# A decoder layer on one NeuronCore: the memory's row factors and mLSTM's gates laid out by DMAs of GpSimd's queue

## The chip, the cores and the metric

The kernel runs on one NeuronCore of a Trainium2 chip, in float32. The metric is the device time of one execution in microseconds (us); a run's time is compared as the median of several.

## What is computed

One decoder layer over 256 tokens of 2048 channels, and a memory of 256 tokens:

```python
h = rms_norm(x, mix_norm_g)
p = h @ w_in                                   # 2048 x 6408, split into ten parts
y_lru = rg_lru_branch(lru_x, lru_z, ...)       # 512 channels
y_ml = mlstm_branch(ml_u, ml_o, ml_z, ml_i, ml_f, ...)  # 4 heads of 192
y_mo = moba_branch(mo_q, mo_k, mo_v, mo_z)     # 6 heads of 128
x = x + concatenate([y_lru, y_ml, y_mo]) @ w_out
x = x + memory_cross_attention(rms_norm(x, xa_norm_g), rms_norm(mem, mem_norm_g), wq, wkv, wo)
return rms_norm(x, final_norm_g)
```

Two pieces matter here. The memory's norm is a factor for each memory token, `rsqrt(mean(mem^2) + eps)`. And mLSTM has an input gate `ig` and a forget gate `lf = log_sigmoid(f)` for each token and head: with `b = cumsum(lf)` and the running maximum of `ig - b`, each score is multiplied by `exp(ig - b - maximum)` of its key and query, and the output is divided by at least `exp(-m)`, where `m` is `b` plus that maximum.

## The kernel before, in words

**The matrix products.** All weights are read once, in 172 chunks, in the order of the table `GROUPS`: lx, u0, u4, lz0, o0, o1, lz2, q0 to q4, k0 to k4, z0, v0, v1, z1, z2, out0 to out3, ck0, ck2, cq0, cq2, cv, wo0 to wo3. A group of 512 or 384 columns has eight chunks of two 128-row tiles, one of 256 columns four chunks of four. `load(i)` fetches chunk i on SyncE's queue (line 172). `split(i)` makes two parts of it: `wh` by ScalarE (line 197) and the remainder `wl` by VectorE (line 198, by the helper of line 148). `mm(i)` multiplies on TensorE: for groups of kind C by pairs of lines 260 (wh) and 261 (wl), for kind X by lines 282 to 284, of which 283 reads wl.

**The order.** The loop of lines 1100 to 1124 writes every engine's order. For chunk i it calls `split(i + 4)`, the next `load`, `mm(i)`, then `done(group)` behind a group's last chunk, then `step()`. `done` puts generators into `queue`, and `step` takes one piece of the generator in front; `urgent` puts one in front, `bg` at the end. `yield HARD` ends a step without anything else. So all work beside the products stands on each engine's queue in the place of the chunk in whose step it was written, and each engine goes through its queue in order.

**The memory's factor.** `mem_stats` (1025) loads `memT`, channels on partitions, in eight pieces. `square` (393) squares each on ScalarE (401), and GpSimd adds the squares up (402, 404). `stats("m")` (417) sums over the partitions by two matmuls with ones (426), takes the power on GpSimd (359), and brings the factors into a row that all partitions have: a diagonal `yt` by VectorE (430), a matmul with ones (433), a copy `rrow` by ScalarE (436). `ck_evac` multiplies by it through `fold` (444): ScalarE copies half of the accumulators to `ev`, VectorE adds the other half, and GpSimd multiplies by `rrow` (451). For x's factor, `xrow_load` and `xrow_square` take row sums from `x` itself. The tile `yt` is used by `x1_evac` too: ScalarE's squares of the output tiles go there (852).

**The gates.** `o_evac` writes the eight gate columns to `if`, tokens on partitions (549). `ml_gates` (555) stands at the end of the queue when o0 is done, and takes its turn in q2. VectorE computes the logarithms in a chain of small instructions on 128 x 8 (561 to 564). Four transposes on TensorE (586, 587) give rows of 4 partitions, one a head, by 256 tokens; VectorE scans them (589, 591); four more transposes (600, 601) bring them back to columns `acol` and `enb`. The negated running maximum goes as two parts to `nrow`, and each head's `scores` (651) broadcasts it to all partitions by two matmuls with `sel` (654), the rows of which choose the head.

**Around the gates.** `ml_conv` (531) has one step a channel tile with three VectorE instructions (537), on `w`; `lru_z` (501) folds the LRU's gate, and ScalarE's Silu (507) reads what GpSimd's fold wrote.

Of the kernel before, what the change touches and what calls it, by code (L numbers as in the profile page):

```python
# [105 lines left out]
def kernel(ctx: ExitStack, tc: tile.TileContext, xT, memT, x, mem, ws, vec_d, lw_d, fg_d, out):  # L106
# [283 lines left out]
    rrow = {}  # L390
    sq = {}

    def square(which, j):

        t = staged[which, j]
        if j == 0:
            sq[which] = small("mask", 512)
            S.activation(sq[which], t.rearrange("p a b -> p (a b)"), AF.Square)
        else:
            q = small("yt", 512)  # L400
            S.activation(q, t.rearrange("p a b -> p (a b)"), AF.Square)  # L401
            G.tensor_tensor(sq[which], sq[which], q, OP.add)  # L402
        if j == 7:
            G.tensor_tensor(sq[which][:, :256], sq[which][:, :256], sq[which][:, 256:], OP.add)

    ssqx = small("ssqx", 2, 2)
    xrow = {}

    def xrow_load(i):
        xrow[i] = big(i + 1, 1024)  # L410
        t, c = i // 2, i % 2 * 1024
        nc.sync.dma_start(xrow[i], x[t * 128:t * 128 + 128, c:c + 1024])

    def xrow_square(i):
        S.activation(xrow[i], xrow[i], AF.Square, accum_out=ssqx[:, i // 2, i % 2:i % 2 + 1])

    def stats(which):
        r = small(f"rstd_{which}", 2)
        rstd[which] = r
        if which == "x":  # L420
            V.reduce_sum(r, ssqx, axis=AX.X)
            rstd_of(r, r, D, RMS_EPS)
        else:
            p = ps()
            for t in range(2):
                P.matmul(p[:, t:t + 1], sq[which][:, t * 128:t * 128 + 128], ones[:, 0:1], start=True, stop=True)
            rstd_of(r, p[:, 0:2], D, RMS_EPS)
        d = small("yt", 512)[:, :256].rearrange("p (a b) -> p a b", a=2)
        for t in range(2):
            V.tensor_scalar(d[:, t, :], ident, r[:, t:t + 1], None, op0=OP.mult)  # L430
        yield
# [122 lines left out]

    def ml_gates():
        iff = M["if"]
        lf, e = small("lf", 8), small("lf_e", 8)
        f = iff[:, :, 4:8]
        e3 = e.rearrange("p (a b) -> p a b", a=2)
        lf3 = lf.rearrange("p (a b) -> p a b", a=2)  # L560
        stt(e3, f, -1.0, f, OP.mult, OP.max)
        S.activation(e, e, AF.Exp, scale=-1.0)
        log1p(lf, e, "lf")
        stt(lf3, f, 0.0, lf3, OP.min, OP.subtract)
        cmask = small("mask", 512)[:, :384]
# [5 lines left out]
        w = big(6, 4, 256)[:4]  # L571
        sel = selp.tile([128, 4, 128], F32R, name="sel")
        ones_r = ones[:, :128]
        M["sel"] = sel
        for h in range(4):
            G.affine_select(sel[:, h, :], ones_r, pattern=[[0, 128]], compare_op=OP.is_equal, fill=0.0,
                            base=-h, channel_multiplier=1)
        nrow = [selp.tile([128, 256], F32R, name=f"nrow{i}") for i in range(2)]
        for r in nrow:
            G.memset(r.bitcast(F32), 0.0)  # L580
        M["nrow"] = nrow
        yield HARD
        yield HARD
        p = ps()
        for t in range(2):
            P.transpose(p[:4, t * 128:t * 128 + 128], lf3[:, t, :], ident)
            P.transpose(p[:4, 256 + t * 128:256 + t * 128 + 128], iff[:, t, 0:4], ident)
        cb, av, cm, ncm = (w[:, i, :] for i in range(4))
        V.tensor_tensor_scan(cb, ones[:4, :], p[:4, 0:256], 0.0, op0=OP.mult, op1=OP.add)
        tt(av, p[:4, 256:512], cb, OP.subtract)  # L590
        V.tensor_tensor_scan(cm, ones[:4, :], av, 0.0, op0=OP.mult, op1=OP.max)
        V.tensor_scalar(ncm, cm, -1.0, None, op0=OP.mult)
        tt(cb, ncm, cb, OP.subtract)
        nh, nl = (r[:4, :] for r in M["nrow"])
        V.tensor_copy(nh, ncm)
        tt(nl, ncm, nh.bitcast(F32), OP.subtract)
        yield HARD
        p = ps()
        for t in range(2):
            P.transpose(p[:, t * 8:t * 8 + 4], av[:, t * 128:t * 128 + 128], ident[:4, :4])  # L600
            P.transpose(p[:, t * 8 + 4:t * 8 + 8], cb[:, t * 128:t * 128 + 128], ident[:4, :4])
        p3 = p[:, :16].rearrange("p (a b) -> p a b", a=2)
        acol, enb = small("acol", 2, 4), small("enb", 2, 4)
        V.tensor_copy(acol, p3[:, :, 0:4])
        S.activation(enb, p3[:, :, 4:8], AF.Exp)
        M["acol"], M["enb"] = acol, enb
        yield HARD

# [35 lines left out]
    def ml_heads():  # L644
# [6 lines left out]
        def scores(h):  # L651
            pn = ps()
            for i in range(2):
                P.matmul(pn[:, :256], M["sel"][:, h, :], M["nrow"][i], start=i == 0, stop=i == 1)
            e = small(f"mo_l{h % 3}", 384)
            E[h] = e
            stt(e[:, :256], pn[:, :256], acol[:, 0, h:h + 1], cmask[:, :256], OP.add, OP.add)
            stt(e[:, 256:], pn[:, 128:256], acol[:, 1, h:h + 1], cmask[:, 256:], OP.add, OP.add)
# [366 lines left out]
    def mem_stats():  # L1025
        for j in range(10):
            if j < 8:
                stage_load("m", memT, j)
            if j >= 2:
                square("m", j - 2)  # L1030
# [9 lines left out]
    def done(name, a):  # L1040
# [59 lines left out]
    for i in range(NS):  # L1100
# [94 lines left out]
```

## Time and profile before

| | |
|---|---|
| median of 3 runs | 522.26 us (521.66 to 522.65) |
| profiled execution | 521.88 us, span 520.2 us |
| TensorE busy (matmuls) | 507.9 us, 98% |
| VectorE, ScalarE, GpSimd busy | 338.0, 292.8, 54.8 us |
| TensorE's granted clock | full in all but the last of 40 slices |
| moved by DMAs | 98.74 MB, 190 GB/s in the mean |

In the profile's rows PE is TensorE's matmuls, PEld its weight loads, DVE is VectorE, ACT ScalarE, POOL GpSimd, SP SyncE, and a q behind a name is that engine's queue of DMA issues. A group of rows below is from the timeline: the start in us from the span's start, the time taken in us, the engine, the line of the kernel, the instruction with what it writes and reads, and how often; in brackets how long the engine stood idle before it and who ended that. TensorE's matmuls overlap, so what one costs is read from the start of the next, not from its own length.

### The profile page before, as it was taken

Reading aid. Unit: us, or ns where it says so; the run is one execution under the profiler, and the core shown is the slowest. Engines: PE = TensorE matmul, PEld = TensorE weight load, DVE = VectorE, ACT = ScalarE, POOL = GpSimd, SP = SyncE. Lnnn points to the kernel's source line nnn. Section 1 sums busy time; section 2 is a strip of 40 time slices with the busy share of each in tenths; the row PEclk is TensorE's granted clock in tenths of the full one; section 3 lists DMA queues with packets and bytes.
Section 4 is the critical chain, followed back from the end, with each engine's and each line's share of the span. In section 5 each row is a group of like instructions: output and inputs, shape, how many; then the busy total and the mean of one; then the engine's idle time right before and its main releaser. Section 6 shows DMA issues by size and latency. Waiting matters only on the chain.

```text
span 520.2 us, 7578 instructions
## 1 busy us (share of the span) xinstructions
PE 507.9 (98%) x2814; PEld 448.8 (86%) x2814; DVE 338.0 (65%) x531; ACT 292.8 (56%) x476; POOL 54.8 (11%) x70
## 2 busy tenths in 40 slices
PE   8999999999999999999999999999999999999993
PEld 6999889998988888889988888888888888888883
DVE  5958848895397656548645466654658749637574
ACT  5775477678544333353545755543649467546353
POOL 2800001000132100002000000000132003000000
PEclk9999999999999999999999999999999999999998
DMA  8995635467446544435843465478575527734704
GB/s 274 360 412 180 187 120 167 139 221 230 160 160 178 186 161 163 151 92 183 271 155 121 137 209 179 164 272 325 188 264 174 194 66 259 237 128 129 234 3 161
DMA packets 31077, 98.74 MB, mean 190 GB/s; under 512 B 3520, under 2 KB 3904, under 8 KB 31040
## 3 DMA queue, kind: packets, MB, share of 16 engines
q1 hardware_dynamic: 30896, 98.25, 56.9%
q8 instruction: 22, 0.36, 0.3%
q14 instruction: 15, 0.12, 0.1%
q10 hardware_dynamic: 144, 0.01, 0.0%
HBM read 96.15 MB, written 2.10 MB: 189 GB/s over the span
## 4 chain that ended last, share of the span: by engine, by line
PE 85%; issue 6%; POOL 3%; DVE 3%; DMA 1%; ACT 1%; SPq 1%; POOLq 0%; ACTq 0%; DVEq 0%
PE acc_out L284 5%; PE acc_out L282 5%; PE acc_out L283 5%; PE acc_q L260 4%; PE acc_k L260 4%; PE acc_z L284 4%; PE acc_z L282 4%; PE acc_z L283 4%; PE acc_cq L260 3%; PE acc_lz L260 3%; PE acc_q L261 2%; PE acc_k L261 2%; PE acc_o L283 2%; PE acc_o L282 2%; PE acc_o L284 2%
## 5 line engine op out<-in xcount | busy, mean ns | idle before, releaser
L148 DVE TENSOR_TENSOR wl<-raw,wh 128x1024 fp32r<-128x1024 f32 (+3 forms) x166 | 199.6, 1212 | 111.7 <-ACT wh L197 109.3
L197 ACT ACTIVATE wh<-raw 128x1024 fp32r<-128x1024 f32 (+2 forms) x162 | 161.8, 1013 | 44.5 <-DMA raw<-ws 14.8
L282 PE MATMUL acc_out<-wh,a_y 128*128 128x512 f32 x128 | 50.8, 397 | 0.0
L284 PE MATMUL acc_out<-wh,a_y 128*128 128x512 f32 x128 | 49.9, 390 | 0.0
L283 PE MATMUL acc_out<-wl,a_y 128*128 128x512 f32 x128 | 49.8, 389 | 0.0
L282 PE MATMUL acc_z<-wh,a_x 128*128 128x512 f32 x96 | 39.6, 412 | 0.0
L284 PE MATMUL acc_z<-wh,a_x 128*128 128x512 f32 x96 | 37.6, 391 | 0.0
L283 PE MATMUL acc_z<-wl,a_x 128*128 128x512 f32 x96 | 37.5, 390 | 0.0
L260 PE MATMUL acc_k<-a_x,wh 128*128 128x512 f32 x96 | 34.4, 401 | 0.0
L260 PE MATMUL acc_q<-a_x,wh 128*128 128x512 f32 x96 | 34.1, 398 | 0.0
L451 POOL TENSOR_TENSOR w<-ev,rrow 128x512 f32<-128x512 f32 x11 | 17.5, 1589 | 153.6 <-DVE ev L148 153.6
L284 PEld LDWEIGHTS acc_out<-wh,a_y 128*128 128x128 f32 x128 | 24.0, 188 | 5.2
L283 PEld LDWEIGHTS acc_out<-wl,a_y 128*128 128x128 f32 x128 | 24.1, 188 | 4.7
L282 PEld LDWEIGHTS acc_out<-wh,a_y 128*128 128x128 f32 x128 | 24.1, 188 | 4.6
L261 PE MATMUL acc_k<-a_x,wl 128*128 128x256 f32 x96 | 26.9, 280 | 0.0
L261 PE MATMUL acc_q<-a_x,wl 128*128 128x256 f32 x96 | 26.8, 280 | 0.0
L402 POOL TENSOR_TENSOR mask<-mask,yt 128x512 f32<-128x512 f32 x7 | 10.3, 1473 | 147.1 <-ACT yt L401 147.1
L260 PE MATMUL acc_lz<-a_x,wh 128*128 128x512 f32 x64 | 23.3, 406 | 0.0
L260 PE MATMUL acc_ck<-a_m,wh 128*128 128x512 f32 x64 | 23.1, 403 | 0.0
L260 PE MATMUL acc_cq<-a_h,wh 128*128 128x512 f32 x64 | 22.7, 399 | 0.0
L283 PE MATMUL acc_o<-wl,a_x 128*128 128x392 f32 (+1 forms) x64 | 21.6, 338 | 0.0
L282 PE MATMUL acc_o<-wh,a_x 128*128 128x392 f32 (+1 forms) x64 | 21.6, 337 | 0.0
(302 smaller groups left out, 1187.4 us busy)
## 6 DMA issues: line engine op xcount, KB each, us to landing
raw<-ws SPq DMA_DIRECT2D x138, 512.0 KB, 4.1
raw<-ws SPq DMA_DIRECT2D x24, 384.0 KB, 3.1
w<-x SPq DMA_DIRECT2D x8, 512.0 KB, 6.5
raw<-ws SPq DMA_DIRECT2D x8, 392.0 KB, 3.1
w<-memT SPq DMA_DIRECT2D x8, 256.0 KB, 6.1
out<-xg SPq DMA_DIRECT2D x8, 256.0 KB, 3.0
w<-xT SPq DMA_DIRECT2D x7, 256.0 KB, 6.7
raw<-ws SPq DMA_DIRECT2D x4, 256.0 KB, 5.0
```

The source lines that it names most:

```text
L148: V.tensor_tensor(out, a, b, op)
L197: S.activation(h[:, :kc * n], r[:, :kc * n], AF.Copy)
L260: P.matmul(a[m], h[:, sl], both, start=first, stop=False, skip_group_check=True)
L261: P.matmul(a[m][:, :256], l[:, sl], xh, start=False, stop=last, skip_group_check=True)
L282: P.matmul(o, xh[:, sl], mh, start=first, stop=False)
L283: P.matmul(o, xh[:, sl], ml, start=False, stop=False)
L284: P.matmul(o, xl[:, sl], mh, start=False, stop=last)
L402: G.tensor_tensor(sq[which], sq[which], q, OP.add)
L451: G.tensor_tensor(dst, e, rb(which), OP.mult)
```

## The change

Three things change.

- The memory's row sums are taken as x's were: four loads of `mem` by rows, 512 KB each, into the tiles w1 and w2, squared by ScalarE with its accumulator (`row_load`, `row_square`). `memT` is still loaded for the products.
- The memory's factors go to DRAM and back: GpSimd's queue writes 256 numbers to `d_m`, three steps later it reads them as a row for all partitions into `rrow`. The diagonal and the matmul are left to x alone.
- `ml_gates` no longer waits in `queue`: it is in `side`, and `step` takes one piece of it in every step. Its two changes of layout go through DRAM on GpSimd's queue: the gates to `d_if` and back as four transfers of four heads by 128 single numbers; the scan's results in four such transfers to `d_gates` and back as `acol`. The maximum goes to `d_nrow` and comes back in `nrow` for all 128 partitions and four heads, 512 KB, so `scores` has no matmul for it. `sel` and the two-part `nrow` go.

```diff
@@ the memory's statistics
-    def square(which, j):
...
-            S.activation(q, t.rearrange("p a b -> p (a b)"), AF.Square)
-            G.tensor_tensor(sq[which], sq[which], q, OP.add)
...
+    MROW = (1, 2, 1, 2)
+
+    def row_load(which, src, i, tag):
+        rows[which, i] = big(tag, 1024)
         t, c = i // 2, i % 2 * 1024
+        nc.sync.dma_start(rows[which, i], src[t * 128:t * 128 + 128, c:c + 1024])
+
+    def row_square(which, i):
+        t = rows[which, i]
+        S.activation(t, t, AF.Square, accum_out=ssq[which][:, i // 2, i % 2:i % 2 + 1])
...
+        V.reduce_sum(r, ssq[which], axis=AX.X)
+        rstd_of(r, r, D, RMS_EPS)
+        rr = small("rrow", 256)
+        if which == "m":
+            yield
+            d = drp.tile([2, 128], F32, name="d_m")
+            with nc.allow_non_contiguous_dma(reason="two numbers a token"):
+                G.dma_start(d.rearrange("t p -> p t"), r)
+            yield from idle(3)
+            G.dma_start(rr, d.rearrange("t p -> (t p)")[None, :].to_broadcast([128, 256]))
         else:
-            p = ps()
-            for t in range(2):
-                P.matmul(p[:, t:t + 1], sq[which][:, t * 128:t * 128 + 128], ones[:, 0:1], start=True, stop=True)
...
@@ the gates, behind the logarithms and the mask
+        V.tensor_copy(f, lf3)
+        yield
+
+        d = drp.tile([256, 8], F32, name="d_if")
+        G.dma_start(d.rearrange("(t p) c -> p t c", t=2), iff)
+        yield from idle(3)
+        w = big(6, 5, 256)[:4]
+        w, o = w[:, :2, :], w[:, 2:, :]
+        with nc.allow_non_contiguous_dma(reason="one number each"):
+            for a in range(2):
+                for n in (slice(0, 128), slice(128, 256)):
+                    G.dma_start(w[:, a, n], d[n, 4 * a:4 * a + 4].rearrange("n h -> h n"))
+        yield from idle(4)
...
+        V.tensor_tensor_scan(cb, ones[:4, :], w[:, 1, :], 0.0, op0=OP.mult, op1=OP.add)
...
+        d, dn = drp.tile([256, 8], F32, name="d_gates"), drp.tile([4, 256], F32, name="d_nrow")
+        with nc.allow_non_contiguous_dma(reason="one number each"):
+            for a in range(2):
+                for n in (slice(0, 128), slice(128, 256)):
+                    G.dma_start(d[n, 4 * a:4 * a + 4].rearrange("n h -> h n"), o[:, a, n])
+        G.dma_start(dn, o[:, 2, :])
+        yield from idle(4)
+        ac, nrow = small("acol", 2, 8), selp.tile([128, 4, 256], F32, name="nrow")
+        G.dma_start(ac, d.rearrange("(t p) c -> p t c", t=2))
+        G.dma_start(nrow, dn[None, :, :].to_broadcast([128, 4, 256]))
+        yield from idle(4)
+        enb = small("enb", 2, 4)
+        S.activation(enb, ac[:, :, 4:8], AF.Exp)
...
@@ scores, step, mem_stats, done
-            pn = ps()
-            for i in range(2):
-                P.matmul(pn[:, :256], M["sel"][:, h, :], M["nrow"][i], start=i == 0, stop=i == 1)
+            pn = M["nrow"][:, h, :]
...
+        for g in list(side):
+            if next(g, True):
+                side.remove(g)
...
+        for j in range(8):
+            if j < 4:
+                row_load("m", mem, j, MROW[j])
+            stage_load("m", memT, j)
+            if 2 <= j < 6:
+                row_square("m", j - 2)
+            yield
...
-            bg(ml_gates())
+            side.append(ml_gates())
```

The scratch for DMAs that the program makes itself (`dynamic_dma_scratch_size`) goes from 2048 to 4096 as well.

**VectorE's order in o1.** The rows are from `if`, the gate columns, on; `w` is the convolution's tile, `lf` and its companions the logarithms. Before:

```order
L151 SCALAR_TENSOR_TENSOR if<-acc_o_1018,rstd_x,vec 128x8
L151 SCALAR_TENSOR_TENSOR if<-acc_o_1019,rstd_x,vec 128x8
L148 TENSOR_TENSOR wl_1180<-raw_1095,wh_1179 128x768
L151 SCALAR_TENSOR_TENSOR w_1150<-w_779,vec,w_1150 128x256 x3
L148 TENSOR_TENSOR wl_1204<-raw_1114,wh_1203 128x768
L151 SCALAR_TENSOR_TENSOR w_1150<-w_779,vec,w_1150 128x256 x3
L148 TENSOR_TENSOR wl_1226<-raw_1136,wh_1225 128x768
L151 SCALAR_TENSOR_TENSOR w_1150<-w_779,vec,w_1150 128x256 x3
```

Now, from the same wl on (lines are those of the changed kernel):

```order
L150 TENSOR_TENSOR wl_1183<-raw_1098,wh_1182 128x768
L153 SCALAR_TENSOR_TENSOR lf_e<-if 128x8
L367 TENSOR_SCALAR lf_q<-lf_e 128x8
L368 RECIPROCAL lf_q<-lf_q 128x8
L150 TENSOR_TENSOR lf_s<-lf_e,lf_q 128x8
L150 TENSOR_TENSOR lf_s_1208<-lf_s 128x8
L371 TENSOR_SCALAR lf_q<-lf_s_1208 128x8
L153 SCALAR_TENSOR_TENSOR lf_q<-lf_q,lf_s_1208 128x8 x6
L153 SCALAR_TENSOR_TENSOR lf_q<-lf_q,lf_s 128x8
L375 TENSOR_SCALAR lf<-lf_q 128x8
L153 SCALAR_TENSOR_TENSOR lf<-if,lf 128x8
L566 COPY if<-lf 128x2x4
```

The logarithms, before written in q2, and a copy of them into `if` stand between the wl of o1's fifth chunk and the convolution's next step; behind the copy the order goes on as before.

**GpSimd's order from lz0 to k0.** `w` with `ev` and `rrow` is a fold; `mask`, `sel` and the first `nrow` are the gates' constants. Before:

```order
L451 TENSOR_TENSOR w_1005<-ev,rrow 128x512
L616 MEMSET qh 64x256 x4
L451 TENSOR_TENSOR w_1005<-ev,rrow 128x512
L451 TENSOR_TENSOR w_1582<-ev,rrow 128x512
L567 MEMSET mask 128x384
L569 AFFINE_SELECT mask<-mask 128x256
L569 AFFINE_SELECT mask<-mask 128x128
L576 AFFINE_SELECT sel<-ones 128x128 x4
L580 MEMSET nrow_1648 128x256
L580 MEMSET nrow_1649 128x256
L451 TENSOR_TENSOR w_1582<-ev,rrow 128x512 x2
```

Now (`w_1322` is the gates' tile of four partitions):

```order
L562 MEMSET mask 128x384
L564 AFFINE_SELECT mask<-mask 128x256
L564 AFFINE_SELECT mask<-mask 128x128
L570 DMA d_if<-if 128x2x8
L577 DMA w_1322<-d_if 4x128x1 x4
L609 MEMSET qh 64x256 x4
L590 DMA d_gates<-w_1322 4x128x1 x4
L591 DMA d_nrow<-w_1322 4x256
L445 TENSOR_TENSOR w_1008<-ev,rrow 128x512
L594 DMA acol<-d_gates 128x2x8
L595 DMA nrow<-d_nrow 128x1024
L445 TENSOR_TENSOR w_1638<-ev,rrow 128x512 x3
```

The gates' DMAs stand in front of the memsets of `qh` (half-filled queries that ScalarE completes) and around lz2's fold (`w_1008` behind `d_nrow`); before, that fold had only `qh` in front of it.

**VectorE's order in out3, the memory's factor.** Before:

```order
L148 TENSOR_TENSOR wl_3922<-raw_3826,wh_3921 128x1024
L151 SCALAR_TENSOR_TENSOR a_m_3939<-w_3707,vec,a_m_3939 128x256 x2
L357 TENSOR_SCALAR rstd_m<-ps_3945 128x2
L430 TENSOR_SCALAR yt<-ident,rstd_m 128x128 x2
L148 TENSOR_TENSOR wl_3954<-raw_3852,wh_3953 128x1024
L151 SCALAR_TENSOR_TENSOR a_m_3971<-w_3707,vec,a_m_3971 128x256 x2
L148 TENSOR_TENSOR w_3482<-acc_out_3764,w_3482 128x512
```

Now:

```order
L150 TENSOR_TENSOR wl_3804<-raw_3700,wh_3803 128x1024
L153 SCALAR_TENSOR_TENSOR a_m_3821<-w_3490,vec,a_m_3821 128x256 x2
L412 TENSOR_REDUCE rstd_m<-ssq_m 128x2
L359 TENSOR_SCALAR rstd_m<-rstd_m 128x2
L150 TENSOR_TENSOR wl_3832<-raw_3719,wh_3831 128x1024
L153 SCALAR_TENSOR_TENSOR a_m_3849<-w_3633,vec,a_m_3849 128x256 x2
L150 TENSOR_TENSOR wl_3857<-raw_3743,wh_3856 128x1024
```

The factor comes four chunks earlier, from ScalarE's sums, and the diagonal in `yt` is gone.

## Rows read from the trace of the kernel before

**Rows 1.** Stretches: us; PE, PEld, DVE, ACT, POOL busy; clock, DMA share, GB/s

```profile
300.00:402.00 102.00, 102.00 (x481) 84.62 (x480) 64.70 (x70) 57.67 (x87) 9.63 (x7) 1.00 0.65 222
```

**Rows 2.** Timeline of TensorE, 149 to 169 us, L586, L600 and L654 between

```profile
149.67 0.28 PE L261 MATMUL acc_q<-a_x,wl 128*128 128x256 f32 x1
150.01 0.28 PE L261 MATMUL acc_q<-a_x,wl 128*128 128x256 f32 x1
...
150.80 0.28 PE L261 MATMUL acc_q<-a_x,wl 128*128 128x256 f32 x1
...
156.10 0.28 PE L261 MATMUL acc_q<-a_x,wl 128*128 128x256 f32 x1
...
156.98 0.28 PE L261 MATMUL acc_q<-a_x,wl 128*128 128x256 f32 x1
...
167.84 0.40 PE L654 MATMUL ps<-nrow,sel 128*128 128x256 f32 x2
168.08 0.59 PE L663 MATMUL ps<-w,w 128*128 128x256 f32 x2
```

**Rows 3.** Timeline of TensorE, 406 to 422 us

```profile
406.69 0.39 PE L283 MATMUL acc_out<-wl,a_y 128*128 128x512 f32 x1
...
407.37 0.39 PE L283 MATMUL acc_out<-wl,a_y 128*128 128x512 f32 x1
...
408.50 0.39 PE L283 MATMUL acc_out<-wl,a_y 128*128 128x512 f32 x1
...
420.47 0.28 PE L261 MATMUL acc_ck<-a_m,wl 128*128 128x256 f32 x1
...
421.25 0.28 PE L261 MATMUL acc_ck<-a_m,wl 128*128 128x256 f32 x1
```

**Rows 4.** Timelines of ScalarE and TensorE around 424 us, [idle before <-releaser]

```profile
421.27 0.63 ACT L852 ACTIVATE yt<-w 128x512 f32<-128x512 f32 x1 [9.16 <-PE ps L433]
...
422.65 1.04 ACT L197 ACTIVATE wh<-raw 128x1024 fp32r<-128x1024 f32 x1
...
423.80 0.46 PE L260 MATMUL acc_ck<-a_m,wh 128*128 128x512 f32 x1
425.01 0.39 PE L261 MATMUL acc_ck<-a_m,wl 128*128 128x256 f32 x1 [0.76 <-DVE wl L148]
```

**Rows 5.** Timelines of VectorE and TensorE, o1 to lz2

```profile
102.18 0.96 DVE L148 TENSOR_TENSOR wl<-raw,wh 128x768 fp32r<-128x768 f32 x1 [1.72 <-ACT wh L197]
...
111.41 1.22 DVE L148 TENSOR_TENSOR wl<-raw,wh 128x1024 fp32r<-128x1024 f32 x1
...
119.98 1.23 DVE L148 TENSOR_TENSOR wl<-raw,wh 128x1024 fp32r<-128x1024 f32 x1 [1.91 <-ACT wh L197]
...
114.06 0.39 PE L260 MATMUL acc_lz<-a_x,wh 128*128 128x512 f32 x1
114.29 0.28 PE L261 MATMUL acc_lz<-a_x,wl 128*128 128x256 f32 x1
```

**Rows 6.** Timeline of VectorE, the gates in q2

```profile
145.28 0.35 DVE L151 SCALAR_TENSOR_TENSOR lf_e<-if 128x8 f32<-128x8 f32 x1
...
149.13 2.35 DVE L148 TENSOR_TENSOR wl<-raw,wh 128x1024 fp32r<-128x1024 f32 x2
151.40 0.67 DVE L589 TENSOR_TENSOR_SCAN w<-ones,ps 4x256 f32<-4x256 f32 x1
```

**Rows 7.** DMA issues: SyncE's timeline; then the list, KB each, us to landing

```profile
1.23 0.42 SPq L169 DMA_DIRECT2D raw<-ws  x1
...
vec<-vec ACTq DMA_DIRECT2D x1, 8.0 KB, 2.2
```

**Rows 8.** Timelines of GpSimd, ScalarE and TensorE, lz2's fold and what follows

```profile
129.44 2.36 POOL L451 TENSOR_TENSOR w<-ev,rrow 128x512 f32<-128x512 f32 x1 [45.08 <-DVE ev L148]
...
131.84 0.63 ACT L507 ACTIVATE w<-w 128x512 f32<-128x512 f32 x1 [1.13 <-POOL w L451]
...
144.81 0.28 PE L261 MATMUL acc_q<-a_x,wl 128*128 128x256 f32 x1
```

More of the change, by code (lines that the diff above doesn't have):

```diff
@@ L15 @@
 PSUM = bass.MemoryType.PSUM
+DRAM = bass.MemoryType.DRAM
 T = 256
@@ L390 @@
     rrow = {}
-    sq = {}
-    def square(which, j):
[L395 to L400, printed above, removed]
-            S.activation(q, t.rearrange("p a b -> p (a b)"), AF.Square)
-            G.tensor_tensor(sq[which], sq[which], q, OP.add)
[L403 to L410, printed above, removed]
+    ssq = {w: small(f"ssq_{w}", 2, 2) for w in "xm"}
+    rows = {}
+    MROW = (1, 2, 1, 2)
+    def row_load(which, src, i, tag):
+        rows[which, i] = big(tag, 1024)
         t, c = i // 2, i % 2 * 1024
-        nc.sync.dma_start(xrow[i], x[t * 128:t * 128 + 128, c:c + 1024])
-    def xrow_square(i):
-        S.activation(xrow[i], xrow[i], AF.Square, accum_out=ssqx[:, i // 2, i % 2:i % 2 + 1])
+        nc.sync.dma_start(rows[which, i], src[t * 128:t * 128 + 128, c:c + 1024])
+    def row_square(which, i):
+        t = rows[which, i]
+        S.activation(t, t, AF.Square, accum_out=ssq[which][:, i // 2, i % 2:i % 2 + 1])
     def stats(which):
@@ L419, in stats @@
         rstd[which] = r
-        if which == "x":
-            V.reduce_sum(r, ssqx, axis=AX.X)
-            rstd_of(r, r, D, RMS_EPS)
-        else:
+        V.reduce_sum(r, ssq[which], axis=AX.X)
[8 more added lines that the diff above has]
+            G.dma_start(rr, d.rearrange("t p -> (t p)")[None, :].to_broadcast([128, 256]))
+        else:
+            d = small("yt", 512)[:, :256].rearrange("p (a b) -> p a b", a=2)
+            for t in range(2):
+                V.tensor_scalar(d[:, t, :], ident, r[:, t:t + 1], None, op0=OP.mult)
+            yield
             p = ps()
-            for t in range(2):
-                P.matmul(p[:, t:t + 1], sq[which][:, t * 128:t * 128 + 128], ones[:, 0:1], start=True, stop=True)
[L427 to L431, printed above, removed]
-        p = ps()
-        P.matmul(p[:, :256], ones[:, :128], d.rearrange("p a b -> p (a b)"), start=True, stop=True)
-        rr = small("rrow", 256)
+            P.matmul(p[:, :256], ones[:, :128], d.rearrange("p a b -> p (a b)"), start=True, stop=True)
+            S.activation(rr, p[:, :256], AF.Copy)
         rrow[which] = rr
-        S.activation(rr, p[:, :256], AF.Copy)
     def rb(which):
@@ L570, in ml_gates @@
                             channel_multiplier=-1)
[L571 to L591, printed above, removed]
@@ L592, in ml_gates @@
-        V.tensor_scalar(ncm, cm, -1.0, None, op0=OP.mult)
-        tt(cb, ncm, cb, OP.subtract)
[L594 to L607, printed above, removed]
+        V.tensor_copy(f, lf3)
+        yield
+        d = drp.tile([256, 8], F32, name="d_if")
[7 more added lines that the diff above has]
+                    G.dma_start(w[:, a, n], d[n, 4 * a:4 * a + 4].rearrange("n h -> h n"))
@@ new lines, in ml_gates @@
+        yield from idle(4)
+        av, cb, ncm = (o[:, i, :] for i in range(3))
+        V.tensor_tensor_scan(cb, ones[:4, :], w[:, 1, :], 0.0, op0=OP.mult, op1=OP.add)
+        tt(av, w[:, 0, :], cb, OP.subtract)
+        V.tensor_tensor_scan(ncm, ones[:4, :], av, 0.0, op0=OP.mult, op1=OP.max)
+        V.tensor_scalar(ncm, ncm, -1.0, None, op0=OP.mult)
+        tt(cb, ncm, cb, OP.subtract)
+        yield
+        d, dn = drp.tile([256, 8], F32, name="d_gates"), drp.tile([4, 256], F32, name="d_nrow")
@@ L609, in ml_qkv @@
+        yield from idle(4)
+        enb = small("enb", 2, 4)
+        S.activation(enb, ac[:, :, 4:8], AF.Exp)
+        M["acol"], M["enb"], M["nrow"] = ac, enb, nrow
+        yield
     def ml_qkv():
@@ L651, in scores @@
         def scores(h):
[L652 to L654 removed]
+            pn = M["nrow"][:, h, :]
             e = small(f"mo_l{h % 3}", 384)
             E[h] = e
[L657 removed]
+            stt(e[:, :256], pn, acol[:, 0, h:h + 1], cmask[:, :256], OP.add, OP.add)
             stt(e[:, 256:], pn[:, 128:256], acol[:, 1, h:h + 1], cmask[:, 256:], OP.add, OP.add)
@@ L996 @@
     queue = deque()
+    side = []
     def bg(*gens):
@@ L1025, in mem_stats @@
     def mem_stats():
[L1026 to L1030, printed above, removed]
+        for j in range(8):
[4 more added lines that the diff above has]
+                row_square("m", j - 2)
             yield
-        yield from idle(2)
         yield from stats("m")
```

7 lines of the change are left out of this document (4 added, 3 removed).

## The prediction

> **What bounds the kernel now.** I read the busy times by stretch first. In the long stretch from 300 to 402 us TensorE is busy for all of it, VectorE and ScalarE for less than two thirds [rows 1]; the stretches from 107 to 500 us look alike but for one hole, at 424 us. So the timeline of TensorE is what must be read: an instruction that leaves it gives back its slot, and every other engine counts only where it lets TensorE wait. It can, because a weight chunk is used only when ScalarE has written its high part (wh) and VectorE its low part (wl), four chunks ahead. Two places matter: how far wl is ahead when the gates are computed, and the hole.
>
> **What leaves TensorE.** Each group is priced by the start of the row behind it, against the same spacing without it.
> - Four transposes into rows (lines 586, 587): L261 to L261 takes 0.34 us undisturbed and 0.79 us with them: 0.45 us [rows 2].
> - Four transposes back (600, 601): 0.88 against 0.34: 0.54 us [rows 2].
> - The maximum's broadcast through `sel` (654): a pair holds 0.24 us until line 663 starts, one pair a head, four heads: 0.96 us [rows 2].
> - The memory's two column sums (426): L283 to L283 is 1.13 us with them and 0.68 without: 0.45 us [rows 3].
> - The memory's factor broadcast (433): 0.78 against 0.34: 0.44 us [rows 3].
>
> Together 2.84 us.
>
> **The hole at 424 us goes too.** ScalarE's squares for the last output tile write `yt`. In the kernel before, `stats("m")` has just put the diagonal for line 433 there, so ScalarE stands idle for 9.16 us until TensorE gets to line 433, and then makes wh of ck2's first chunk only at 422.65 us [rows 4]. TensorE starts that chunk at 423.80 us, and its first wl matmul, usually 0.23 us behind (as from 114.06 to 114.29 us [rows 5]), comes at 425.01 us, waiting on wl [rows 4]. That is 1.21 - 0.23 = 0.98 us. After the change nothing of the memory's statistics touches `yt` or TensorE, so the wait has no cause left. What is late next is nothing there: ScalarE is 9 us ahead of where it was.
>
> **What the gates' new place costs.** The log-sigmoid chain moves on VectorE from q2 (145 us) to right behind wl of o1's fifth chunk. There it takes 149.13 - 145.28 = 3.85 us for 15 instructions, 0.26 each [rows 6]; the new copy makes a sixteenth: 4.1 us. In the old place TensorE shows no wait behind it, so its leaving gives nothing. In the new place VectorE is full. From 102.18 us on it alternates three convolution steps with one wl and has no idle mark until behind lz2's second wl; TensorE uses up an o1 chunk a little faster than that, and the lead is gone when lz2 begins: lz2's first wl runs from 111.41 to 112.63 us, and TensorE wants it at 114.29 us [rows 5]. With 4.1 us in front it is done at 116.73 us. TensorE waits 116.73 - 114.29 = 2.44 us, in pieces over o1 and lz2. Later chunks have wider leads, so it is paid once. Between ends: nothing, if VectorE's 1.72 us of idle ahead of 102.18 us [rows 5] and something else unseen take it, and 4.1 us, if the lead were nil; I take 2.44, which both rows give directly.
>
> **The DMAs of GpSimd's queue.** No row of this trace shows one. There are two kinds. Contiguous ones (`d_if`, `d_nrow`, `acol`, `nrow`, `rrow`) I price like the other queues' issues: 0.42 us to issue one over 128 partitions, and 2.2 us to landing for ScalarE's 8 KB [rows 7]. The eight in between move 512 single numbers each (four heads by 128 tokens). Low end: 0.42 us each, if pieces don't matter. By pieces, at SyncE's 0.42 us for 128 rows: 1.7 us. High end: GpSimd's own pace, 2.36 us for 512 columns of a fold beside a busy VectorE [rows 8], doubled for one read and one write of each piece: 4.7 us. I take 1.7 us, an estimate nearest to an actual DMA issue.
>
> What they may cost hangs on three waits. First: the copy ends near 102.18 + 0.96 + 4.1 = 107.2 us, `d_if` has landed at about 110, the four reads at 110 + 4g + 2.2 for an issue of g. VectorE comes to the scan behind wl of lz2's step, 119.98 + 1.23 + 4.1 = 125.3 us [rows 5]; the reads are there if g is under 3.3 us. (`qh`'s memsets stand behind the reads' issues; ScalarE writes that tile in the same steps, so its bound is this one.) Second: lz2's fold on GpSimd now stands behind the four writes and `d_nrow`, ScalarE's Silu waits for the fold, and wh and wl of q2's second chunk stand behind the Silu. TensorE wants that wl at 144.81 [rows 8] + 2.44 = 147.2 us; back over wl 1.22, wh 1.04, Silu 0.63 and fold 2.36, the fold must start by 142.0 us. The scan's five instructions, each no longer than the 0.67 us of the first [rows 6], are through by 125.3 + 3.4 = 128.7; with 0.4 us for `d_nrow`, four writes fit if g is under 3.2 us. Third: `acol` and `nrow` are issued behind the fold, land some 6 us later and are first read four chunk steps on, by the exponential on ScalarE (eight pairs of 0.34 us a chunk, 11 us). At 1.7 us an issue all three are covered and the cost is nothing.
>
> First the rows: SyncE needs 0.42 us for 128 pieces, which says nothing on how GpSimd makes 512. The Trainium skill, page "DMA: Bandwidth & Descriptors", section "Rules for kernel authors", says that a last dimension that isn't contiguous turns into one descriptor per element and should be rearranged; it speaks against the eight small transfers. By it the issue is 1.7 us or more rather than 0.42; the sum stays as it is up to 3.2 us, and the rival below takes the rest.
>
> **Edits at nothing.** Four squares of 1024 columns replace eight of 512 and their GpSimd additions; the four loads of 512 KB more are 2.1 MB in a stretch that moves 222 GB/s at a DMA share of 0.65 [rows 1], so about 20 GB/s more, with TensorE without a wait there. If that cover were gone, a late wh would show as idle TensorE in out0. SyncE waits for the first two squares before it reloads their tiles; the weight loads behind have four chunks of lead. `d_m` and `rrow` run behind out3's start and are first read by ck0's fold, ten microseconds or more later.
>
> **Sum.** Against the profiled execution, 521.88 us (span 520.2): -2.84 - 0.98 + 2.44 = -1.38, so 520.5 us. The median of the runs, 522.26, is 0.38 us above that execution; from it I get 520.9 us.
>
> **Rivals.**
> - *Nothing stalls in o1.* VectorE's chain hides after all, and the full 3.82 us stay: 518.4 us. For it: the lead is only read from one execution. Against: the stretch has no idle VectorE to take 4.1 us.
> - *GpSimd's queue becomes the bound.* If an issue of 512 single numbers takes over 3.3 us, the reads reach the scan late and the writes hold the fold, the Silu and wh: each microsecond beyond costs TensorE eight, four in the reads and four in the writes. It is slower than before from g = 3.5 us on (1.38 / 8 = 0.17 beyond 3.3). At the high end of 4.7 us: 520.9 + 8 x 1.4 = 532.1 us. For it: GpSimd is slow per column, and the chain has four hops. Against: the estimate is half of that. The skill's rule above is the mechanism's reason.
> - *A wash.* The stall in o1 is nearer its upper end, because ScalarE takes an exponential into the same place and wh comes late too; at the full 4.1 us the sum is -2.84 - 0.98 + 4.1 = +0.28: 522.5 us.
> - *The change doesn't do what it says* can be left out: the order of the changed program has none of the five groups on TensorE.
>
> **How the numbers follow.** Forecast 0.42 (519.9 to 521.2 us), no stall in o1 0.14, a wash 0.18, GpSimd's queue 0.26. About 0.2% (1.0 us) is what a measurement can tell from no change; it lies close to the forecast. Faster takes the forecast and the first rival, less 0.03 at the forecast's upper edge: 0.53. Same takes the wash, that edge and 0.01 of GpSimd's queue just beyond 3.3 us: 0.22. Slower is the rest of GpSimd's queue: 0.25. The range goes from the first rival's 518.4, with 0.2 for the measurement, to 530.0 us (g near 4.4 us): it leaves out about half of the last rival and little below. The forecast's own range, 519.9 to 521.2 us, takes the wait in o1 from 1.4 to 2.7 us.
>
> **What would show it.** Right: TensorE's rows without the five groups; waits on wl in o1 and lz2's first chunk of some 2.4 us in all, with the log chain in front; no wait of ScalarE on line 433 and no hole at ck2; GpSimd's small issues under 3 us; no wait of the scan on a DMA that TensorE feels. Wrong: TensorE idle in q0 to q2 with the scan, the Silu or the gates' exponential waiting for GpSimd or its DMAs; no wait at all in o1; idle TensorE in out0 from the memory's loads.

## The result, and the profile after

The changed kernel takes 543.55 us (median of 4 runs, 540.8 to 544.93) against 522.45 us for the kernel before in the same session: a ratio of 1.040, with a 95% interval of 1.0356 to 1.0443. It is slower by 21 us; the forecast was 520.9 us, the range ended at 530.0. The profiled execution spans 543.2 us, against 520.2.

The page after (busy us and share; then busy tenths in 40 slices of 13.6 us, TensorE's and its granted clock's):

```profile
PE 511.8 (94%) x2792; PEld 451.1 (83%) x2792; DVE 335.6 (62%) x528; ACT 293.4 (54%) x476; POOL 55.1 (10%) x70
...
PE   7999999998557999999999999999999989999994
...
PEclk8999999999786999999999999999999999999998
```

TensorE is busy for 94% of the span (98% before); what it lost lies nearly all in the three slices from 136 to 177 us (the digits 5, 5 and 7). Outside them the page is nearly like the page before; the 8 at 435 to 448 us is taken up with the memory's factors below. The clock falls in the same place. The stretch view shows it closer (us; PE, PEld, DVE, ACT, POOL busy; clock, DMA share, GB/s):

```profile
137.00:141.00 4.00, 0.00 (x0) 0.00 (x0) 3.86 (x7) 0.00 (x0) 1.09 (x1) 0.68 0.15 1
141.00:145.00 4.00, 3.71 (x12) 3.22 (x13) 4.00 (x6) 0.00 (x0) 0.00 (x0) 0.50 0.33 30
...
158.00:162.00 4.00, 0.00 (x0) 0.00 (x0) 0.00 (x0) 0.00 (x0) 0.11 (x1) 0.62 0.05 0
162.00:166.00 4.00, 0.00 (x0) 0.00 (x0) 0.00 (x0) 1.15 (x2) 2.81 (x3) 0.50 0.39 3
166.00:170.00 4.00, 3.05 (x8) 2.26 (x9) 2.58 (x3) 4.00 (x9) 1.07 (x2) 0.50 0.50 35
```

From 158 to 162 us almost nothing runs: TensorE, VectorE and ScalarE stand still, and the weights' DMAs have stopped too (0 GB/s). All of them wait for one queue. GpSimd's timeline (start, us, instruction, in brackets the idle time before it and what ended it):

```profile
110.36 1.16 POOL L577 DMA_DIRECT2D w<-d_if  x1 [1.87 <-ACT w L529]
117.10 1.12 POOL L577 DMA_DIRECT2D w<-d_if  x1 [5.59 <-issue]
124.62 1.09 POOL L577 DMA_DIRECT2D w<-d_if  x1 [6.40 <-issue]
131.73 1.10 POOL L577 DMA_DIRECT2D w<-d_if  x1 [6.01 <-issue]
...
138.47 1.09 POOL L590 DMA_DIRECT2D d_gates<-w  x1 [4.23 <-DVE w L150]
146.23 1.10 POOL L590 DMA_DIRECT2D d_gates<-w  x1 [6.67 <-issue]
155.05 1.09 POOL L590 DMA_DIRECT2D d_gates<-w  x1 [7.73 <-issue]
161.89 1.10 POOL L590 DMA_DIRECT2D d_gates<-w  x1 [5.75 <-issue]
162.97 0.56 POOL L591 DMA_DIRECT2D d_nrow<-w  x1
163.55 1.27 POOL L445 TENSOR_TENSOR w<-ev,rrow 128x512 f32<-128x512 f32 x1
```

The four reads (577) and the four writes (590) each last 1.1 us, but they start 7.1 us (21.37 / 3) and 7.8 us (23.42 / 3) apart, and between them GpSimd waits for nothing that the profile names ("issue"). But the first read lands 6.40 us after its start, at 116.76 us, and the second starts at 117.10; the second and third land at 124.32 and 131.42, and the next ones start at 124.62 and 131.73. Each starts 0.3 us after the one before has landed, and so do the writes (landed at 145.92, 154.75 and 161.58). What hangs on these DMAs is the chain that the prediction laid out, on VectorE and on ScalarE:

```profile
136.94 0.68 DVE L580 TENSOR_TENSOR_SCAN w<-ones,w 4x256 f32<-4x256 f32 x1 [11.62 <-DMA w<-d_if]
```

```profile
164.85 0.63 ACT L501 ACTIVATE w<-w 128x512 f32<-128x512 f32 x1 [31.51 <-POOL w L445]
```

The scan waits 11.6 us for the last read; wl of q0's second chunk stands behind the scan. The Silu (501) waits 31.5 us for lz2's fold, which stood at 129.44 us before [rows 8] and comes at 163.55 us now, behind the writes; wh of q2's second chunk stands behind the Silu. TensorE (first matmuls of the two stalled chunks and the pairs behind them):

```profile
133.34 0.40 PE L262 MATMUL acc_q<-a_x,wh 128*128 128x512 f32 x1
141.29 0.58 PE L263 MATMUL acc_q<-a_x,wl 128*128 128x256 f32 x1 [7.55 <-DVE wl L150]
141.67 0.63 PE L262 MATMUL acc_q<-a_x,wh 128*128 128x512 f32 x1
...
142.32 0.63 PE L262 MATMUL acc_q<-a_x,wh 128*128 128x512 f32 x1
```

```profile
156.71 0.28 PE L263 MATMUL acc_q<-a_x,wl 128*128 128x256 f32 x1
166.48 0.80 PE L262 MATMUL acc_q<-a_x,wh 128*128 128x512 f32 x1 [9.50 <-ACT wh L199]
...
168.12 0.63 PE L262 MATMUL acc_q<-a_x,wh 128*128 128x512 f32 x1
...
168.76 0.63 PE L262 MATMUL acc_q<-a_x,wh 128*128 128x512 f32 x1
...
172.60 0.39 PE L262 MATMUL acc_q<-a_x,wh 128*128 128x512 f32 x1
...
172.94 0.40 PE L262 MATMUL acc_q<-a_x,wh 128*128 128x512 f32 x1
```

It waits 7.55 us for wl and 9.50 us for wh. The second thing to see is the spacing of the wh matmuls behind each wait: 0.64 us (168.12 to 168.76), where it is 0.34 us later (172.60 to 172.94) and was 0.34 before, from wl to wl [rows 2]. The granted clock is 0.50 there, the lower of the two levels, and full again 4 to 6 us after work resumes. In numbers: q0's second chunk takes 13.68 us from start to start (133.34 to 147.02) against 4.08 before, 9.60 more, of which 7.55 is the wait. q2's first two take 18.55 us (154.05 to 172.60) against 5.55 before, 13.0 more, of which 9.50 is the wait. So 22.6 us in all, 17.05 of waiting; the other 5.5 us are in the main the half clock that follows each wait (0.46 us is a second, short wait for wl at 167.74 us).

### The profile page after: what moved, and what is told of

It reads as the page before. It is cut to its first block, busy times and chain, and to the rows that moved or that the text cites. A ratio compares the mean times of both kernels' runs of the same rounds, so it can differ in the third digit from the quotient of the medians.

```text
span 543.2 us, 7552 instructions
## 1 busy us (share of the span) xinstructions
PE 511.8 (94%) x2792; PEld 451.1 (83%) x2792; DVE 335.6 (62%) x528; ACT 293.4 (54%) x476; POOL 55.1 (10%) x70
## 4 chain that ended last, share of the span: by engine, by line
PE 78%; issue 10%; DMA 4%; ACT 3%; DVE 3%; POOL 2%; SPq 0%; ACTq 0%; POOLq 0%; DVEq 0%
PE acc_out L286 5%; PE acc_out L284 5%; PE acc_out L285 5%; PE acc_k L262 4%; PE acc_z L286 4%; PE acc_z L285 4%; PE acc_z L284 4%; DMA raw<-ws 3%; PE acc_cq L262 3%; PE acc_q L262 3%; PE acc_ck L262 2%; PE acc_k L263 2%; PE acc_v L285 2%; PE acc_v L286 2%; PE acc_v L284 2%
## 5 line engine op out<-in xcount | busy, mean ns | idle before, releaser
L150 DVE TENSOR_TENSOR wl<-raw,wh 128x1024 fp32r<-128x1024 f32 (+3 forms) x166 | 197.4, 1202 | 120.7 <-ACT wh L199 116.6
L262 PE MATMUL acc_q<-a_x,wh 128*128 128x512 f32 x96 | 38.3, 435 | 9.5 <-ACT wh L199 9.5
L263 PE MATMUL acc_q<-a_x,wl 128*128 128x256 f32 x96 | 29.1, 303 | 8.0 <-DVE wl L150 8.0
L262 PEld LDWEIGHTS acc_q<-a_x,wh 128*128 128x128 f32 x96 | 20.1, 209 | 14.5 <-ACT wh L199 9.8
L263 PEld LDWEIGHTS acc_q<-a_x,wl 128*128 128x128 f32 x96 | 20.2, 210 | 8.8 <-DVE wl L150 8.8
```

The costliest lines, as they stand in the source:

```text
L150: V.tensor_tensor(out, a, b, op)
L262: P.matmul(a[m], h[:, sl], both, start=first, stop=False, skip_group_check=True)
L263: P.matmul(a[m][:, :256], l[:, sl], xh, start=False, stop=last, skip_group_check=True)
```

## The experiments

All ratios are to the kernel before, run beside. The first question was which part costs what: the memory's factors, the maximum through DRAM, or the single-number DMAs, and why these stand 7 us apart.

**The memory's factors alone.** `ml_gates` and `scores` are those of before:

```
-            side.append(ml_gates())
+            bg(ml_gates())
```

> The memory's factors as in the changed kernel (row sums on ScalarE, the factor row through DRAM), the gates and heads as in the kernel before. The prediction's terms for this part alone are 0.45 + 0.44 us of TensorE's groups and 0.98 us of the wait at the start of ck2's first chunk, so its theory expects 1.9 us less than before (ratio about 0.9964, near 520.4 us). Rival: the two DMAs (the trace after has GpSimd waiting 10.9 us for the first to land) hold ck0's fold, and the part is worth nothing or costs time (ratio 1.000 or over). If 1.9 us is right, the gates alone cost the changed kernel about 23 us.

520.03 us (5 runs), ratio 0.9956 (0.9944 to 0.9969): 2.3 us less, 1.9 foreseen. ScalarE's squares of the last output tile, which stood idle for 9.16 us [rows 4], now wait for their own data only:

```profile
413.95 0.63 ACT L846 ACTIVATE yt<-w 128x512 f32<-128x512 f32 x1 [1.15 <-DVE w L150]
```

ck2's first chunk takes 2.83 us from start to start on TensorE, 3.90 before. So the whole loss, and 2.3 us more, belongs to the gates.

The rival's DMAs are late in this run too, but not for the fold: `d_m` lands 9.3 us after its start, and ck0's fold, at 424.98 us, waits for VectorE's sums (`ev`). What suffers is the weights. `d_m` is 256 single numbers on their way to DRAM, and the six weight chunks issued from 398 to 414 us land in 3.2 to 10.0 us here, in 3.2 to 4.1 before. In this run the lead covers it: ck0's first chunk takes 3.18 us, 3.48 before. In the trace after it doesn't:

```profile
d_m<-rstd_m POOLq DMA_DIRECT2D x1, 1.0 KB, 11.4
```

```profile
434.57 1.06 ACT L199 ACTIVATE wh<-raw 128x1024 fp32r<-128x1024 f32 x1 [2.31 <-DMA raw<-ws]
```

There the four chunks issued beside `d_m` land in 10.4 to 11.5 us, wh waits for one of them, and ck0's first chunk takes 5.37 us, 1.9 more than before.

**The maximum through DRAM, with whole rows.** On top of it:

```
-        V.tensor_copy(nh, ncm)
-        tt(nl, ncm, nh.bitcast(F32), OP.subtract)
+        G.dma_start(dn, ncm)
...
+        G.dma_start(nrow, dn[None, :, :].to_broadcast([128, 4, 256]))
```

> The memory's factors as changed, and of the gates only the running maximum: the transposes on TensorE and the log-sigmoid stay where they were before, but the maximum of four rows goes to DRAM and back to all partitions by two DMAs with whole rows, so the four pairs of selection products leave TensorE. Prediction's terms: 0.45 + 0.44 + 0.98 + 0.96 = 2.8 us less than before (ratio about 0.9946, near 519.5 us). Rival: the round trip through DRAM comes late and scores wait for it, with a time above that of the kernel with the memory's part alone.

518.82 us (5 runs), 0.9934 (0.9922 to 0.9947): 1.2 us less than the memory's part alone, 0.96 foreseen; the two intervals just overlap. On TensorE the chunks of the first three heads' scores (the first ones of k0, k2 and k4) take 0.18 to 0.23 us less than in the run before, 0.24 foreseen for each head. A round trip through DRAM by GpSimd's queue is no harm in itself.

**More room for GpSimd's DMAs.** The changed kernel with

```
-    nc = bacc.Bacc("TRN2", target_bir_lowering=False, num_devices=1, dynamic_dma_scratch_size=4096)
+    nc = bacc.Bacc("TRN2", target_bir_lowering=False, num_devices=1, dynamic_dma_scratch_size=10240)
-        ac, nrow = small("acol", 2, 8), selp.tile([128, 4, 256], F32, name="nrow")
+        ac, nrow = small("acol", 2, 8), big(6, 4, 256)
```

> The changed kernel with the scratch for GpSimd's DMAs raised from 4096 to 10240 bytes; to make room the broadcast maximum takes the buffer that the gates leave (4 KB of another pool). Theory ring: each single-number DMA waits until the one before it has left the scratch, so only one is under way at a time, 7 us apart. With 2.5 times the room several are issued behind one another at about 1.1 us each; the scan starts near 125 us instead of 137, lz2's fold no later than 150 instead of 163.6, and the time falls by 15 us or more, to 519 to 529 us. Theory making: GpSimd needs some 7 us to make 512 pieces whatever room there is; spacing and time stay as in the changed kernel, 543 us within 2.

524.72 us (5 runs), 1.0044 (1.0029 to 1.006). 18.8 of the 21 us are gone. Four DMAs now go out in one row of GpSimd's timeline:

```profile
110.84 4.43 POOL L577 DMA_DIRECT2D w<-d_if  x4 [1.88 <-ACT w L529]
...
133.65 4.33 POOL L590 DMA_DIRECT2D d_gates<-w  x4 [16.96 <-DVE w L150]
```

So GpSimd makes 512 pieces in 1.1 us; the theory of slow making falls, and the 7 us were a wait for room. But the eight DMAs are not free now. ScalarE's waits from 100 to 160 us (what waits for what, us in all, times, longest):

```profile
ACT wh L199 <- DMA raw<-ws: 16.7, 5, 4.7
```

Before, this wait was 1.1 us in that stretch. A read takes 10.9 us from issue to landing, a write 12.7, and the weights come late beside them, beside the reads as well: the longest of the five waits, 4.7 us, ends at 126.52 us, before the first write is issued, and from 116 to 120 us all transfers together move 57 GB/s (240 before).

**Less room than that.** The same with 8192.

> As ring10k with 8192 bytes of scratch. In the changed kernel (4096) one single-number DMA is under way at a time, with 10240 all four went out 1.1 us apart. If a DMA takes over half of 4096 and over a quarter but at most a third of 8192, three go out 1.1 us apart and the fourth 5 us or more later, in the reads and in the writes alike; the time is then between ring10k's 524.7 and the changed kernel's 543.5, nearer to the first: 526 to 534 us. Rival: spacing is no matter of the scratch's room, and with 8192 the four go out as with 10240 or as with 4096.

```profile
110.44 3.35 POOL L577 DMA_DIRECT2D w<-d_if  x3 [1.88 <-ACT w L529]
118.79 1.10 POOL L577 DMA_DIRECT2D w<-d_if  x1 [5.00 <-issue]
...
131.10 3.25 POOL L590 DMA_DIRECT2D d_gates<-w  x3 [9.80 <-DVE w L150]
138.63 1.10 POOL L590 DMA_DIRECT2D d_gates<-w  x1 [4.28 <-issue]
```

Three go out together and the fourth 5 us (reads) and 4.3 us (writes) later, as foreseen to the count; the fourth read starts at 118.79 us, 0.34 us after the first has landed. One DMA in 4096 bytes, three in 8192, four in 10240: each takes between 2048 (8192 / 4, which doesn't fit) and 2560 bytes (10240 / 4). The Trainium skill, page "DMA: Bandwidth & Descriptors", sections "Terms" and "Why a DMA increments its semaphore by 16 and not by 1", has descriptors of 16 bytes and lets the outermost dimension set how many DMA engines share a transfer; with four partitions that would be four engines and, an estimate, 128 pieces and one closing entry on each: 129 x 16 = 2064 bytes. The runs agree with it. The time missed the expectation on the good side: 521.32 us (10 runs), 0.9995 (0.9983 to 1.0008), 3.4 us less than with 10240. With three in flight the scan comes at 129.6 us, with four at 132.1, both times right behind a wl that was late; what differs is how many are under way beside the weights, and that this sets the time is argued. The weight chunks issued from 110 to 125 us land in 4.1 us before (median), in 5.0 in the changed kernel with one read in flight, in 9.1 here; with four it is 8.8, and the slowest takes 11.7 (9.8 here).

**The fold off GpSimd's queue.** The changed kernel with lz0's and lz2's folds finished by VectorE:

```
-            G.tensor_tensor(dst, e, rb(which), OP.mult)
+            E.tensor_tensor(dst, e, rb(which), OP.mult)
...
-        fold(dst, a, "x")
+        fold(dst, a, "x", V)
```

> The changed kernel with the second step of lz0's and lz2's fold on VectorE instead of GpSimd, so the Silu no longer stands behind GpSimd's four single-number writes. The reading that the writes cost TensorE their time through this fold alone (chunks 48 and 49, 9.7 and 3.4 us over before) expects 13 us less than the changed kernel, about 530 us; what is left over before is then the reads in front of the scan (chunk 45, 9.6 us). Rival: another wait behind GpSimd's queue (the arriving gates, 178 us) or VectorE's own order takes its place, and the gain is under 5 us.

536.23 us (4 runs), 1.027 (1.0255 to 1.0286). It gained 7.3 us, not 13. The wait at q2's first two chunks is gone (2.77 us each, as before), but the queue's next customer stepped into its place, ScalarE's exponential of the gates' columns (598), with q4's wh behind it (ScalarE's waits from 160 to 190 us):

```profile
ACT enb L598 <- DMA acol<-d_gates: 13.3, 1, 13.3
```

That was the prediction's third wait. A queue that is late is not mended by taking one customer out of it.

**ScalarE's queue.** The changed kernel with `G.dma_start` replaced by `S.dma_start` on the eight lines.

> The changed kernel with its eight single-number DMAs issued from ScalarE's queue, which doesn't use GpSimd's scratch. If GpSimd's scratch is all, they go out without 7 us between them and the time is that of ring10k or below, 520 to 525 us. Rival: the pieces themselves are slow wherever they are issued, or making 512 pieces holds ScalarE's own instructions up (wh, and TensorE behind it), and the time stays over 530 us.

526.0 us (4 runs), 1.0071 (1.0057 to 1.0085), just over the upper edge of the first theory. No 7 us pauses, but ScalarE itself is held:

```profile
109.23 9.42 ACTq L577 DMA_DIRECT2D w<-d_if  x4
...
130.77 8.80 ACTq L590 DMA_DIRECT2D d_gates<-w  x4
```

2.2 to 2.4 us for each DMA of 512 numbers, in which it makes no wh: lz2's first chunk takes 7.31 us on TensorE, 3.45 before. This queue's packets are counted: 4272 in the whole run, 144 in the trace after, so 516 for each of the eight DMAs, which is 4 x 129, the count of the estimate above.

**The log-sigmoid in o1, without such DMAs.** On top of m_nrow, the chain becomes a generator of its own:

```
+            side.append(ml_log())
             bg(ml_gates())
```

> The kernel m_nrow with one part of the change more: the log-sigmoid chain is done beside o1 as in the changed kernel, not in q0's stretch. No single-number DMA is in it. The prediction's term for the chain on VectorE in o1 is 2.44 us of waiting (bounds 0 to 4.1), which would give 518.8 + 2.4 = 521.3 us; what the trace after shows at chunks 37 to 40 is 2.1 us, which gives 520.9. Rival: the time comes back later, since q0's and q2's stretch is relieved of the chain, and the kernel stays within 0.5 us of m_nrow.

520.78 us (11 runs), 0.9975 (0.9966 to 0.9984): 2.0 us more than m_nrow. On TensorE it lies where the prediction put it: o1's last three chunks take 3.10, 2.33 and 2.31 us (2.08 each before) and lz2's first 3.90 (3.45), 1.95 us in all. Nothing comes back later.

**Four writes that nobody waits for.** On top of m_nrow, with 10240 bytes, four DMAs like line 590's into a DRAM tile that nothing reads; `d_if`'s whole-row write is there too, landed by 149 us.

> The kernel m_nrow with four single-number DMAs more, to DRAM, of the same form as the changed kernel's writes, whose result nothing reads, issued where GpSimd has little to do (near 160 us), with 10240 bytes of scratch; the gates' numbers lie in other buffers, which moves nothing. Theory that such pieces hold the weights' transfers up: a late raw and a wait of TensorE of 1 to 3 us after 160 us (in the ring10k run chunk 50 is 1.9 us over), so 520 to 522 us. Rival: only what waits for such a DMA costs time; then the kernel is within 0.5 us of m_nrow's 518.8.

519.08 us (5 runs), 0.9945 (0.9931 to 0.9959). The difference to m_nrow is within the intervals: the rival's case. Yet the weights are held up. ScalarE's waits from 155 to 185 us, then the DMA issues from 155 to 180 us (KB each, median us to landing):

```profile
ACT wh L199 <- DMA raw<-ws: 6.1, 2, 5.4
```

```profile
raw<-ws SPq DMA_DIRECT2D x8, 512.0 KB, 8.7
...
d_gates<-mo_p POOLq DMA_DIRECT2D x4, 2.0 KB, 13.0
```

A weight chunk lands in 8.7 us, where m_nrow's median in the same stretch is 4.4, and wh waits up to 5.4 us. TensorE doesn't notice, since wl of k0 to k2 is ready 6.7 to 9.9 us ahead there. So the delay is real, and the lead decides whether it costs. In ring10k the lead had been used up by the log chain and by the weights that came late beside the reads.

**Turning over 128 partitions.** The changed kernel, 4096 bytes, turned transfers only where 128 partitions take part:

```
-                    G.dma_start(w[:, a, n], d[n, 4 * a:4 * a + 4].rearrange("n h -> h n"))
+                G.dma_start(d[:, t * 128:t * 128 + 128].rearrange("c p -> p c"), iff[:, t, :])
...
-                    G.dma_start(d[n, 4 * a:4 * a + 4].rearrange("n h -> h n"), o[:, a, n])
+                G.dma_start(ac[:, t, :], d[:, t * 128:t * 128 + 128].rearrange("c p -> p c"))
```

> The changed kernel with its 4096 bytes of scratch and the same gates through DRAM, but the turning is done where 128 partitions take part: the gates' numbers go to DRAM turned, from 128 partitions, in two DMAs of 1024 numbers, and are read back as whole rows; the results go out as whole rows and come back turned, to 128 partitions, in two DMAs. Twice the numbers per DMA, half as many DMAs. Theory that room in the scratch goes by the numbers on each of the 16 DMA engines, and that a DMA over 4 partitions uses few of them: two such DMAs fit beside each other, they go out about 1.2 us apart, and the time is that of ring8k or below, 519 to 523 us. Rival: room goes by the count of numbers whatever the partitions; then one DMA of 1024 doesn't fit at once, the second goes out 7 us or more after the first, and the time is over 525 us.

528.7 us (6 runs), 1.0123 (1.0104 to 1.0142). On the room the theory held: both DMAs of 1024 numbers go out in 2.00 us with 4096 bytes.

```profile
107.84 2.00 POOL L572 DMA_DIRECT2D d_if<-if  x2 [22.75 <-DVE if L566]
```

On the time it failed, and for another reason than the rival gave. The stretch view (columns as above), and ScalarE's next wh:

```profile
108.00:112.00 4.00, 3.06 (x18) 2.65 (x16) 3.89 (x7) 2.07 (x4) 1.83 (x2) 1.00 0.96 12
112.00:116.00 4.00, 4.00 (x22) 3.57 (x21) 3.86 (x9) 0.00 (x0) 0.00 (x0) 1.00 0.30 27
116.00:120.00 4.00, 3.78 (x20) 2.80 (x19) 2.38 (x4) 0.00 (x0) 0.00 (x0) 1.00 0.65 32
120.00:124.00 4.00, 0.00 (x0) 0.00 (x0) 0.00 (x0) 0.83 (x1) 1.84 (x5) 0.93 0.90 299
```

```profile
123.17 1.06 ACT L199 ACTIVATE wh<-raw 128x1024 fp32r<-128x1024 f32 x1 [13.10 <-DMA raw<-ws]
```

While the 2048 single numbers are on their way to DRAM, from 108 to 120 us, all transfers together move 12 to 32 GB/s (208 to 240 before), with the DMA engines busy for up to 0.96 of a stretch. wh of lz2's second chunk waits 13.1 us for its raw, and lz2's first two chunks take 11.26 and 4.80 us on TensorE (3.45 and 3.68 before): its matmuls of line 612 wait 6.4 us for ScalarE's Silu of line 534, which stands behind that wh. The four weight chunks issued from 106 to 122 us land in 10.9 to 13.2 us. The turned reads on the way back do no such thing (KB each, median us to landing), and TensorE is busy for all of the stretch from 140 to 160 us in which they run; the six weight chunks issued from 136 to 150 us land in 3.4 to 5.8 us:

```profile
d_if<-if POOLq DMA_DIRECT2D x2, 4.0 KB, 11.3
acol<-d_gates POOLq DMA_DIRECT2D x2, 4.0 KB, 5.0
```

**The best of it.** m_nrow with the second transposes through DRAM too: whole rows out, turned reads to 128 partitions; the gates' exponential waits for the first scores.

```
+        G.dma_start(d.rearrange("(a h) n -> h a n", a=2), w[:, :2, :])
...
+                G.dma_start(ac[:, t, :], d[:, t * 128:t * 128 + 128].rearrange("c p -> p c"))
```

> The kernel m_nrow with the second transposes of the gates through DRAM as well: two whole-row writes, two turned reads to 128 partitions, the log-sigmoid and the first transposes as before. TensorE is spared 0.54 us (prediction's price of this group), so 518.3 us if the columns land before the first scores (168 us; they are written near 154). Rival: they land after that, or GpSimd's queue holds q2's or q4's fold while it waits to read them, and the time is 519 us or more.

518.16 us (5 runs), 0.9927 (0.9915 to 0.9939), the fastest of all. Against m_nrow's 0.9934 the gain is not certain; the direction and size fit the 0.54 us. m_nrow and m_cols both beat the kernel before (by 3.5 and 3.8 us) and the changed one.

## Why the prediction was wrong, step by step

- **The step that failed is the price of a single-number DMA**, g: "by pieces, at SyncE's 0.42 us for 128 rows: 1.7 us", between 0.42 and 4.7. GpSimd is busy for 1.1 us with one, below the value taken; but at 4096 bytes of scratch the next can't start until this one has landed, so the queue moves at 7.1 and 7.8 us a DMA, above the upper end. The bound was built from what an issue costs the engine. The time for the pieces to land, which sets the pace once the room is full, had no term.
- **The mechanism was the rival "GpSimd's queue becomes the bound"**, at 0.26 with an end of 532.1 us. Its two conditions came true in place: the scan late behind the reads, the fold, the Silu and wh late behind the writes. Its slope of eight for each microsecond of g doesn't hold: (7.1 - 3.3) x 4 + (7.8 - 3.2) x 4 = 34 us, where TensorE lost 22.6. Four DMAs have three gaps, and the first pause moves the second deadline back, which the two sums of four took as independent.
- **The clock was not in any step.** 5.5 of the 22.6 us are mainly matmuls at the lower clock behind each pause. A wait of 7.55 us cost 9.60, one of 9.50 cost 13.0.
- **The other terms held.** The memory's groups and the hole: 0.45 + 0.44 + 0.98 = 1.9 foreseen, 2.3 measured (0.0044 of 522.3, give or take 0.7); the hole itself 1.07 against 0.98. The maximum's selection products: 0.96 foreseen, 1.2 measured, with intervals that overlap. The log chain in o1: 2.44 foreseen, 2.0 measured. The first transposes' 0.45 us stands in no run by itself, and the second ones' 0.54 is not certain (m_cols). 22.6 + 2.0 - 2.3 - 1.2 = 21.1 us, the loss of the medians; this is near, not exact, since the 22.6 us are from a trace whose run is 1.4 us over its median, and the transposes and ck0 are left out.
- **The sum without the queue** is ring8k, as near as these runs come to it: 521.3 us against the forecast of 520.9. It isn't quite free of the DMAs (the fourth still waits 5 us, weights still come late), so this agreement is in part luck.
- **Not all of the edits at nothing stayed so.** The memory's loads and squares did: TensorE is busy for all of the stretch from 280 to 430 us in the trace after. `d_m` didn't. The prediction asked only whether the factors are there in time for ck0's fold, and they are; it had no term for what 256 single numbers do to the weights beside them, 1.9 us at ck0 in the trace after. In m_only's trace the lead covers it.

What stays open: why single numbers on their way hold the weights' reads up. That they do is shown beside writes (dummy4w, row_layout, `d_m` in m_only and after) and beside reads to 4 partitions (ring10k, ring8k); beside reads to 128 partitions (row_layout, m_cols) it isn't seen. Where they meet was not tried, and for reads no two runs differ in the partitions alone.

## What to carry to other kernels

Price a DMA by two numbers: what it costs the queue that issues it, and how long its pieces take to land; with little scratch GpSimd's queue moves at the second. Of the small turned transfers tried here only reads to 128 partitions left the weights alone, so that is where to put the turning; 256 numbers written to DRAM one by one are enough to make weights late. Rows that are whole can go through DRAM for almost nothing. Before putting anything on a queue in front of work that others wait for, list all customers behind it, and ask how much lead each still has.

## What was not expected of the hardware

- GpSimd issues 512 pieces in 1.1 us, but starts the next such DMA only when there is room, 0.3 us after an earlier one has landed: one in 4096 bytes of scratch, three in 8192, four in 10240 for four partitions; two of 1024 numbers over 128 partitions in 4096.
- ScalarE's own queue is held for 2.2 to 2.4 us by the same 512 pieces.
- 2048 single numbers written to DRAM took 11.3 us to land (median of the two DMAs) and pressed the core's whole traffic to 12 to 32 GB/s; the same count read from DRAM to 128 partitions took 5.0 us, beside weights that came in time.
- 256 single numbers are enough: beside `d_m` in the trace after four weight chunks landed in 10.4 to 11.5 us, and in the same place before in 3.2 to 4.1.
- More DMAs in flight were worse than fewer: 524.7 us with four, 521.3 with three.
- After a pause of 7.5 to 9.5 us TensorE ran for 4 to 6 us at 0.50 of its clock, so that the two waits cost 27% and 37% more than themselves (a short second wait is in the 37%).
